# Two layers of a four-mixer decoder trunk: array quarters in C, token forms by TensorE, GpSimd's products on VectorE, and a new instruction order

## The chip, the cores and the metric

The kernel runs on one core of a Trainium2 chip. The metric is the device time of one execution in microseconds (us), the median of several runs. The engines are TensorE (PE in the profile; its weight loads are PEld), VectorE (DVE), ScalarE (ACT), GpSimd (POOL) and SyncE (SP), which issues the DMAs.

## The reference, cut to what matters

Two post-norm layers work on x of 512 tokens by 1024 channels, in float32. One input projection feeds four mixers that stand side by side, each with four heads of 64 channels:

```python
for l in range(DEPTH):                                   # DEPTH = 2
    h = x @ w_in[l]
    o_a = gated_deltanet(...)    # A: conv, chunks of 64, triangular inverse, scan over 8 chunks
    o_b = mla(...)               # B: latent attention, causal softmax, 128-query blocks
    o_c = hgrn2(...)             # C: S_t = diag(f_t) S_{t-1} + (1-f_t) i_t^T, o_t = S_t^T q_t
    o_d = dilated_attention(...) # D: (window, dilation) = (128,1), (512,4), (2048,16), ALiBi
    mixed = concat(o_a, o_b, o_c, o_d) @ w_out[l]
    x = layer_norm(ALPHA * x + mixed)
    x = layer_norm(ALPHA * x + W2 @ square(relu(W1 @ x)))
```

C, linear attention with a decay for each channel, is what the change touches most. Its scores within a chunk of 64 tokens are sums over channels of q_t k_s times the product of the f between s and t.

## The kernel before, in words

**Layout.** Activations are held with channels on the 128 partitions and the 512 tokens along the row. A head has 64 channels, so a row tile holds two heads, called a pair; `p` is 0 or 1 for the two pairs of a mixer, and `half[h]` is the half of the partitions of head `h` in its pair.

**Two kinds of matmul.** Projections, the output projection and the feed-forward go through `mm3` (line 558): each operand is split into a high and a low part of type fp32r (`split`, line 544: ScalarE copies the high part, VectorE subtracts), and three matmuls of 512 columns make one product. All else is plain fp32, for which the trace has two records of a matmul, and one of a transpose.

**An order made by a planner.** Every operation is recorded by `Plan.record` (line 263) and placed by `Plan.order` (line 310), a simulation on the host with costs for each operation, a bias for each stream and engine (`BIAS`), a limit of buffers (41 rows of 128x512, eight PSUM banks) and costs for a change of TensorE's tile form (`LEAVE`, `ENTER`). What comes out is the order in which each engine runs its instructions; an engine's order is strict, so an instruction that waits holds up those behind it. All instructions are emitted from one line, so every row of the profile says L472 and one goes by tile names.

**Mixers.** `a_proj` (line 736) makes A's q, k, v and gate. `to_tokens` (line 587) turns a row tile into its token form, tokens of a chunk on the partitions: eight VectorE transposes of 32x32 blocks, 32 partitions each. It is called for A's v and k (`vtok`, `ktok`) and for C's value and key (`vt`, `kt`). A's triangular inverse is a chain of small VectorE operations (`LB`, `TB`, `W`), spread into `T` and `U` and finished by 64x64 matmuls; `quads` (line 582) writes such a set of sixteen, chunk by chunk, head by head. Since operands and output of head `h` lie on `half[h]`, a set uses two of the array's four 64x64 quarters, those on the diagonal.

C (from line 1047) goes pair by pair, streams C0 and C1. Its scores are made in seven levels, and between levels q and k are multiplied by decay products (`qa` on VectorE, `kr` and `tot` on GpSimd):

```python
quads(p, lambda n, s: pe.matmul(o[s, n], lhsT=v3(kr[p])[s, n], rhs=v3(qa[p])[s, n],
                                start=True, stop=True))
ve.copy_predicated(v3(sc[p]), rep(ci[:, i]), scores())
ve.tensor_tensor(qv[:, :, 1], qv[:, :, 1], spread(tv[:, :, 0], b), OP.mult)
po.tensor_tensor(kv[:, :, 0], kv[:, :, 0], spread(tv[:, :, 1], b), OP.mult)
```

`attend` (line 1152) does one pair of heads and one block of 128 queries in B and D: scores, softmax, transposes on TensorE (`tt`), and value products `out[half[h]]`, 128 rows by 64 columns of the array for each head. In D a score is two fp32r matmuls: `dq` with `dk`, which holds the high part of a head on one half and the low part on the other, on all 128 rows; then the low part of q (`dl`) with `dk` on the head's own 64 rows.

GpSimd does single products of two SBUF tiles: `qd`, `dt`, `db`, `N`, `kd` and the scan's state `st` in A, `t1` and `t2` in B, `fl`, `kr` and `tot` in C, `gm` in `gated` (line 616).

Of the kernel before, what the change touches and what calls it, by code (L numbers as in the profile page):

```python
# [159 lines left out]
class Plan:  # L160
# [4 lines left out]
    TO_PE = 70.0  # L165
    LEAVE, ENTER = 95.0, {(128, 128): 105.0}
    WINDOW, DOWN, UP = 3413.0, 0.29, 0.65

    def __init__(self, nc):
        self.nc, self.ops, self.tiles = nc, [], 0  # L170
        self.kinds, self.queues, self.stream, self.bias = {}, {}, "", 0
        self.quota, self.reserve, self.fifo = {}, {}, set()
        self.ties, self.tied = {}, None
# [33 lines left out]
    def cost(self, e, method, out, ins, k):  # L207
        n = math.prod(out.shape[1:])
        psum = any(v.buf.kind == "ps" for v in [out, *ins])
        if e == "pe":  # L210
            if method == "transpose":
                return 109.0
            w, x = k["lhsT"], k["rhs"]
            n, m = math.prod(x.shape[1:]), w.shape[1]
            if w.dt == FR:
                return max(n * 0.4167 + 13.5, 109.0)
            t = 2 * max(2 * n * 0.4167 + 3, 2 * min(m, n) * 0.4167 + 3, 25.0)
            if w.shape[0] <= 64 or m <= 64:
                return t - 12 if out.span()[0] < 64 else 12.0
            return t  # L220
# [26 lines left out]

    def tile_of(self, method, k):
# [5 lines left out]
        return grid(k["lhsT"].shape[0]), grid(k["lhsT"].shape[1])  # L254

# [7 lines left out]
    def record(self, e, method, a, k):  # L263
# [8 lines left out]
        ins = [v for v in [*a[1:], *k.values()] if isinstance(v, View) and not any(v is o for o in outs)]  # L272
# [32 lines left out]
        if self.tied is not None and e.name == "pe":  # L305
            self.tied.append(i)
        self.ops.append([e, method, a, k, deps, list(bufs.values()), cost, tail, i + self.bias + BIAS.get((self.stream, e.name), 0),
                         self.activity(e, method, k, cost), self.tile_of(method, k)])

    def order(self):  # L310
# [18 lines left out]
        warm, dense, mode, run, forced = False, True, None, 0, None  # L329
# [44 lines left out]
        while done < n:  # L374
            best = None
            for e, cand in avail.items():
                pick = None
                for i in cand if forced is None or e != "pe" else (forced,):
                    t = max(at[e], ready[i])
                    new = [b for b in ops[i][5] if not b.held]  # L380
# [8 lines left out]
                    turn = e == "pe" and mode is not None and ops[i][10] != mode  # L389
                    if turn and at[e] - ready[i] < PATIENCE:  # L390
# [10 lines left out]
            t = max(at[e], ready[i])  # L401
            for kd in {b.kind for b in new}:
# [10 lines left out]
            if e == "pe":  # L413
# [5 lines left out]
                if not warm:  # L419
                    cost, work = 2 * cost, 2 * work  # L420
                if mode is not None and op[10] != mode:
                    t = max(t, at[e] + self.LEAVE)
                    cost += self.ENTER.get(op[10], 50.0)
                mode, forced = op[10], self.ties.get(i)
                run = run + 1 if op[9] >= DENSE else 0
                busy += work
                gap = math.exp(-(t - at[e]) / EMA)
# [3 lines left out]
            at[e] = t + cost  # L431
            self.warm[i] = warm
            end[i] = at[e]
# [9 lines left out]
            for j in users[i]:  # L443
# [6 lines left out]
                ready[j] = max(ready[j], end[i] + lat)  # L450
# [24 lines left out]
def emit(ctx, tc, io, layers=DEPTH):  # L475
# [117 lines left out]

    def tables(first, n, name):
# [14 lines left out]
    for l in range(layers):  # L609
# [6 lines left out]
        def gated(ot, gate, gain, k, tag):  # L616
# [7 lines left out]
            po.tensor_tensor(m, ot, sq, OP.mult)  # L624
# [108 lines left out]
        kq = [big("kq", [128, 8, 2, 64]) for _ in range(2)]  # L733
        vtok, z = [None, None], [None, None]
        bx = row("bx")
        def a_proj(name, o=None):
# [31 lines left out]
            dst = kq[p][:, :, 1 if name[1] == "q" else 0, :]  # L768
# [83 lines left out]
        for p in range(2):  # L852
# [10 lines left out]
            po.tensor_tensor(v3(qd[p]), kq[p][:, :, 1, :], v3(eg), OP.mult)  # L863
# [4 lines left out]
            po.tensor_tensor(v3(dt), v3(dt), rep(incl), OP.mult)  # L868
            db = row("db")
            po.tensor_tensor(v3(db), v3(dt), spread(beta[:, :, p]), OP.mult)  # L870
            QK[p] = row("QK")
            for nh in range(2):
                o = ps("a", (128, 4, 2, 64))
                for i in range(4):
                    for h in range(2):
                        b = kq[p][half[h], 4 * nh + i]
                        pe.matmul(o[half[h], i], lhsT=b[:, 0, :], rhs=b, start=True, stop=True)
# [14 lines left out]
        sq1 = row("bsq1")  # L892
# [6 lines left out]
        ac.activation(cq[1][lo], bx[lo], AF.Copy, scale=pcol(P_GQ + 1, lo))  # L899
        ac.activation(sq1[lo], bx[lo], AF.Square)  # L900
        s = ps("a")
        total(s, oner, [sq, sq1[lo]])
# [3 lines left out]
        for h in range(4):  # L906
# [3 lines left out]
            pe.matmul(o, lhsT=wuq[1][lo, hs], rhs=cq[1][lo], start=False, stop=True)  # L910
# [13 lines left out]
        r = slice(64, 96)  # L924
        t1 = row("t1")
        t2 = row("t2")
        po.tensor_tensor(t1[r], bx[r], qtab[r], OP.mult)
        po.tensor_tensor(t2[r], bx[r], ktab[r], OP.mult)
        o = ps("b")
        pe.matmul(o, lhsT=kdup[r], rhs=t1[r], start=True, stop=False)  # L930
        pe.matmul(o, lhsT=krot[r], rhs=t2[r], start=False, stop=True)
# [44 lines left out]
        for p in range(2):  # L976
# [3 lines left out]
            po.tensor_tensor(Nv, pn(LT, p), rep(lev), OP.mult)  # L980
# [21 lines left out]
            to_tokens(v3(ktok), kq[p][:, :, 0, :])  # L1002
            ve.tensor_tensor(v3(ke), v3(ktok), spread(ce[:, 0, :, p]), OP.mult)
            po.tensor_tensor(v3(kd[p]), v3(ktok), spread(ce[:, 1, :, p]), OP.mult)
# [8 lines left out]
        for n in range(8):  # L1013
# [28 lines left out]
            else:  # L1042
                po.tensor_tensor(new, st, spread(ce[:, 2, n]), OP.mult)
# [22 lines left out]
        for name in W_TILES[9:17]:  # L1066
# [4 lines left out]
            if name[1] == "f":  # L1071
# [4 lines left out]
                po.tensor_tensor(fl, fl, e, OP.add)  # L1076
# [8 lines left out]
            elif name[1] == "i":  # L1085
# [3 lines left out]
                to_tokens(v3(vt[p]), v3(t))  # L1089
# [5 lines left out]

        ot = [row("ot"), row("ot")]
        for p in range(2):
            def scores():
                o = ps("b", (128, 8, 64))
                quads(p, lambda n, s: pe.matmul(o[s, n], lhsT=v3(kr[p])[s, n], rhs=v3(qa[p])[s, n],  # L1100
                                                start=True, stop=True))
                return o
            plan.stream = f"C{p}"
            sc[p] = row("sc")
            ve.tensor_tensor(v3(sc[p]), scores(), rep(id64), OP.mult)
            ve.tensor_tensor(qa[p], qa[p], f[p], OP.mult)
            tot = f[p]
            for i in range(6):
                b = 1 << i
                if i < 4:  # L1110
                    ve.copy_predicated(v3(sc[p]), rep(ci[:, i]), scores())
                else:
                    o = ps("b", (128, 8, 64))
                    parts = [(a, slice(a, a + b), slice(a + b, a + 2 * b)) for a in range(0, 64, 2 * b)]
                    quads(p, lambda n, s: [pe.matmul(o[s.start + a:s.start + a + b, n, cq], lhsT=v3(kr[p])[s, n, ck],
                                                     rhs=v3(qa[p])[s, n, cq], start=True, stop=True)
                                           for a, ck, cq in parts])
# [4 lines left out]
                nb = S // (2 * b)  # L1122
                qv = qa[p].rearrange("q (n s b) -> q n s b", s=2, b=b)
                kv = kr[p].rearrange("q (n s b) -> q n s b", s=2, b=b)
                tv = tot.rearrange("q (n s) -> q n s", s=2)
# [3 lines left out]
                po.tensor_tensor(nt_, tv[:, :, 0], tv[:, :, 1], OP.mult)  # L1129
                tot = nt_  # L1130
            kt = row("kt")
            to_tokens(v3(kt), v3(kr[p]))
            ds_ = ps("b", (128, 8, 64))
            quads(p, lambda n, s: n < 7 and pe.matmul(ds_[s, n], lhsT=v3(kt)[s, n], rhs=v3(vt[p])[s, n],
# [294 lines left out]
```

## Time and profile before

| what | us |
|---|---|
| median of 3 runs | 1382.39 (1381.54 to 1384.11) |
| the profiled execution's own time | 1383.82 |
| its span, first to last instruction | 1382.0 |
| TensorE busy in the span | 1336.3 |
| VectorE busy | 784.7 |
| ScalarE busy | 596.7 |
| GpSimd busy | 91.4 |

The profiled execution has 1.8 us outside the span. In the rows, "busy" joins overlapping instructions. A record of TensorE lasts until its modelled end, so records overlap, and the time that one costs is seen from the start of one to the start of the next. TensorE's granted clock was 0.985 of full speed on average; it has two levels, 2.4 GHz (1.00 in the rows) and 1.2 GHz (0.50).

The mixers of the first layer take the span from about 0 to 297 us, its output projection and feed-forward from there to 669 us; the second layer repeats this from 669 us.

### The profile page before, as it was taken

To read this page: it belongs to the slowest core of one execution; us is meant where nothing else is said; L and a number is where in the kernel's file an instruction comes from. 1 tells how busy PE (TensorE), PEld (TensorE's weight loads), DVE (VectorE), ACT (ScalarE), POOL (GpSimd) and SP (SyncE) were. 2 spreads that over 40 slices of the span, in tenths; PEclk is the share of its full clock that TensorE was granted. 3 is DMA by queue.
4 is the path that set the end of the run, shared out by engine and by line. 5 is a ranking of instruction groups with operands and counts; after the bars stand their busy time and mean duration, and the time that the engine had idled before them with its cause. 6 is when DMAs were issued, how large, how long until landed. Compare 5 with 4: busy or idle time off the path is not lost.

```text
span 1382.0 us, 21797 instructions
## 1 busy us (share of the span) xinstructions
PE 1336.3 (97%) x8860; PEld 1084.0 (78%) x8860; DVE 784.7 (57%) x1533; ACT 596.6 (43%) x1124; POOL 91.4 (7%) x108
## 2 busy tenths in 40 slices
PE   8899999999999999999998989999999999999997
PEld 7657778778888888888886678787788888888886
DVE  6989585567743334422479898846658333344226
ACT  6643456548432223321485434656374322233112
POOL 0222020010000000000003212200000000000000
PEclk9999999999999999999999999999999999999999
DMA  6122201232542223324122242021415323232341
GB/s 225 40 88 77 82 4 47 77 122 74 165 141 93 92 92 94 105 92 155 59 92 62 92 146 71 3 69 69 135 64 189 116 92 92 92 106 92 126 149 61
DMA packets 44164, 132.65 MB, mean 96 GB/s; under 512 B 4896, under 2 KB 5152, under 8 KB 44064
## 3 DMA queue, kind: packets, MB, share of 16 engines
q1 hardware_dynamic: 44064, 131.27, 29.5%
q8 instruction: 69, 1.13, 0.3%
q14 instruction: 31, 0.25, 0.1%
HBM read 122.86 MB, written 8.39 MB: 95 GB/s over the span
## 4 chain that ended last, share of the span: by engine, by line
PE 76%; DVE 14%; ACT 7%; issue 2%; DMA 1%; POOL 0%; SPq 0%; DVEq 0%; POOLq 0%; ACTq 0%
PE mm L472 42%; PE a L472 17%; PE b L472 16%; ACT lny L472 2%; DVE wl L472 1%; DVE xt L472 1%; DVE y L472 1%; ACT wh L472 1%; DVE vtok L472 1%; PE o L472 1%; DVE ktok L472 1%; ACT scr L472 1%; ACT sg L472 1%; ACT xH L472 1%; DVE X L472 1%
## 5 line engine op out<-in xcount | busy, mean ns | idle before, releaser
L472 DVE TENSOR_TENSOR wl<-wr,wh 128x1024 fp32r<-128x1024 f32 (+1 forms) x195 | 237.6, 1222 | 360.4 <-ACT wh L472 355.1
L472 ACT ACTIVATE wh<-wr 128x1024 fp32r<-128x1024 f32 (+1 forms) x195 | 204.7, 1054 | 528.6 <-PE mm L472 501.1
L472 PE MATMUL mm<-xH,wl 128*128 128x512 f32 (+1 forms) x832 | 328.0, 395 | 0.0
L472 PE MATMUL mm<-xL,wh 128*128 128x512 f32 (+1 forms) x832 | 326.6, 393 | 0.0
L472 PE MATMUL mm<-xH,wh 128*128 128x512 f32 (+1 forms) x832 | 325.7, 392 | 0.7 <-DVE as L472 0.4
L472 PEld LDWEIGHTS mm<-xH,wh 128*128 128x128 f32 x832 | 157.9, 190 | 38.1 <-issue 1.9
L472 PEld LDWEIGHTS mm<-xL,wh 128*128 128x128 f32 x832 | 157.5, 190 | 38.1 <-issue 2.3
L472 PEld LDWEIGHTS mm<-xH,wl 128*128 128x128 f32 x832 | 157.6, 190 | 34.8 <-issue 1.6
L472 DVE TENSOR_TENSOR hL<-h,hH 128x512 fp32r<-128x512 f32 x64 | 41.8, 687 | 73.4 <-PE mm L472 73.2
L472 PE MATMUL b<-wh,hL 128*128 128x512 f32 x192 | 74.8, 390 | 0.0
L472 PE MATMUL b<-wh,hH 128*128 128x512 f32 x192 | 74.8, 390 | 0.0
L472 PE MATMUL a<-wh,hH 128*128 128x512 f32 x192 | 74.8, 389 | 0.0
L472 PE MATMUL a<-wl,hH 128*128 128x512 f32 x192 | 74.8, 389 | 0.0
L472 PE MATMUL b<-wl,hH 128*128 128x512 f32 x192 | 74.7, 389 | 0.0
L472 PE MATMUL a<-wh,hL 128*128 128x512 f32 x192 | 74.7, 389 | 0.0
L472 PE MATMUL mm<-wh,hH 128*128 128x512 f32 x128 | 49.9, 390 | 0.0
L472 PE MATMUL mm<-wh,hL 128*128 128x512 f32 x128 | 49.8, 389 | 0.0
L472 PE MATMUL mm<-wl,hH 128*128 128x512 f32 x128 | 49.8, 389 | 0.0
L472 ACT ACTIVATE at<-at,as 128x512 f32<-128x512 f32 (+3 forms) x64 | 35.7, 558 | 27.6 <-DVE as L472 27.5
L472 ACT ACTIVATE hH<-h 128x512 fp32r<-128x512 f32 x64 | 37.3, 619 | 15.4 <-DVE h L472 15.2
L472 DVE TENSOR_TENSOR h<-h,mm 128x512 f32<-128x512 f32 x60 | 40.6, 680 | 3.6 <-ACT h L472 3.6
L472 PEld LDWEIGHTS a<-wl,hH 128*128 128x128 f32 x192 | 36.1, 188 | 7.6
(292 smaller groups left out, 2275.8 us busy)
## 6 DMA issues: line engine op xcount, KB each, us to landing
wr<-in_w_ff_dram SPq DMA_DIRECT2D x128, 512.0 KB, 3.6
wr<-in_w_in_dram SPq DMA_DIRECT2D x47, 512.0 KB, 3.6
wr<-in_w_out_dram SPq DMA_DIRECT2D x16, 512.0 KB, 3.6
x<-xt SPq DMA_DIRECT2D x24, 256.0 KB, 2.1
xt<-x SPq DMA_DIRECT2D x24, 256.0 KB, 5.8
ln<-in_ln_dram SPq DMA_DIRECT2D x16, 256.0 KB, 5.5
x<-in_xT_dram SPq DMA_DIRECT2D x8, 256.0 KB, 6.1
dtab<-in_tabs_dram SPq DMA_DIRECT2D x8, 256.0 KB, 4.0
```

The lines of the kernel that those rows point to most:

```text
L472: getattr(e.real, method)(*[real(v) for v in a], **{n: real(v) for n, v in k.items()})
```

## The change

Six edits:

1. `turn` takes the place of `to_tokens`: four TensorE transposes of 128x128 into one PSUM bank, and four ScalarE copies of 64 partitions by 256 elements out of it. For pair 1 of C the two heads are put on crossed halves.
2. C works both pairs in step. `four` writes a set of matmuls for both pairs, in the order chunk, pair, head, with pair 1's output on the other half of the partitions; `together` ties the set into one uninterrupted run of TensorE. The read-out is split in two: a set with the scores, copied by ScalarE, and for each pair a set with the state, added by VectorE.
3. Value products of a block in `attend` are tied into one run by `together`.
4. D's second score matmul takes all 128 rows: the low part of q is kept once per head and copied to both halves by ScalarE. In B the up-projection of q and the rotary products take 128 rows, and the two squares are added by VectorE ahead of one `total`.
5. All `po.tensor_tensor` become `ve.tensor_tensor`; GpSimd keeps its memsets.
6. The planner has other constants and a finer model: quarters of the array that are free on their own, a port that VectorE and GpSimd share, 21 biases in the place of 4. The order of all instructions is new.

```diff
-FILL = (0.3, 0.5)
-EMA = 2000.0
-BURST = 2
-PATIENCE = 2000.0
+FILL = (0.1, 0.4)
+EMA = 3000.0
+BURST = 4
+PATIENCE = 1000.0
-BIAS = {('A0', 'ac'): -50, ('B', 've'): 600, ('C0', 've'): 200, ('D', 'ac'): -200}
+BIAS = {('', 've'): -550, ('A', 'ac'): 400, ('A', 'po'): 1400, ('A', 've'): -25, ('A0', 'ac'): -250,
...
+    def turn(dst, src, tag, crossed=0):
+        o = ps(tag, (128, NT, 128))
+        for m in range(NT):
+            pe.transpose(o[:, m], src[:, 128 * m:128 * m + 128], ident)
+        d = dst.rearrange("q (m c) i -> q m c i", c=2)
+        for h in range(2):
+            for c in range(2):
+                ac.activation(d[half[h ^ crossed], :, c], o[half[c], :, 64 * h:64 * h + 64], AF.Copy)
...
-                to_tokens(v3(vtok[p]), v3(y))
+                turn(v3(vtok[p]), y, "a")
...
-            po.tensor_tensor(v3(qd[p]), kq[p][:, :, 1, :], v3(eg), OP.mult)
+            ve.tensor_tensor(v3(qd[p]), kq[p][:, 1], v3(eg), OP.mult)
...
+        ve.tensor_tensor(sq[lo], sq[lo], sq1[lo], OP.add)
         s = ps("a")
-        total(s, oner, [sq, sq1[lo]])
+        total(s, oner, [sq])
...
-            pe.matmul(o, lhsT=wuq[1][lo, hs], rhs=cq[1][lo], start=False, stop=True)
+            pe.matmul(o, lhsT=wuq[1][:, hs], rhs=cq[1], start=False, stop=True)
...
-        for p in range(2):
-            def scores():
-                o = ps("b", (128, 8, 64))
-                quads(p, lambda n, s: pe.matmul(o[s, n], lhsT=v3(kr[p])[s, n], rhs=v3(qa[p])[s, n],
-                                                start=True, stop=True))
-                return o
...
+        def four(tags, fn, chunks=8):
+            o = [ps(tags, (128, 8, 64)) for p in range(2)]
+            with plan.together():
+                for n in range(chunks):
+                    for p in range(2):
+                        for h in range(2):
+                            fn(o[p], p, n, half[h], half[h ^ p])
+            return o
+
+        def level(o, p, n, s, x):
+            pe.matmul(o[x, n], lhsT=v3(kr[p])[s, n], rhs=v3(qa[p])[s, n], start=True, stop=True)
...
+                for p, o in enumerate(four("b", level)):
+                    ve.copy_predicated(v3(sc[p]), rep(ci[:, i]), o)
...
-                po.tensor_tensor(kv[:, :, 0], kv[:, :, 0], spread(tv[:, :, 1], b), OP.mult)
+                ve.tensor_tensor(kv[:, :, 0], kv[:, :, 0], spread(tv[:, :, 1], b), OP.mult)
...
+        inner = four("b", lambda o, p, n, s, x: pe.matmul(
+            o[s, n], lhsT=v3(vt[p])[x, n], rhs=v3(sc[p])[x, n], start=True, stop=True))
+        for p in range(2):
+            ac.activation(ot[p], inner[p].rearrange("q n i -> q (n i)"), AF.Copy)
             o = ps("b", (128, 8, 64))
+            quads(p, lambda n, s: n and pe.matmul(o[s, n], lhsT=sv[p][s, n], rhs=v3(qa[p])[s, n], start=True, stop=True))
+            ve.tensor_tensor(v3(ot[p])[:, 1:], v3(ot[p])[:, 1:], o[:, 1:], OP.add)
...
-            for j in range(n + 1):
-                for h in range(2):
-                    pe.matmul(out[half[h]], lhsT=vv[j // 2][:, j % 2, 64 * h:64 * h + 64], rhs=tt[h][:, 128 * j:128 * j + 128],
-                              start=j == 0, stop=j == n)
+            with plan.together():
+                for j in range(n + 1):
+                    for h in range(2):
+                        pe.matmul(out[half[h]], lhsT=vv[j // 2][:, j % 2, 64 * h:64 * h + 64],
+                                  rhs=tt[h][:, 128 * j:128 * j + 128], start=j == 0, stop=j == n)
...
-                    ve.scalar_tensor_tensor(dl[p][a], o[a], -0.125, t[a].bitcast(FT), op0=OP.mult, op1=OP.subtract)
+                    r = dl[2 * p + h] = row("dl", FR)
+                    ve.scalar_tensor_tensor(r[a], o[a], -0.125, t[a].bitcast(FT), op0=OP.mult, op1=OP.subtract)
+                    ac.activation(r[b], r[a].bitcast(FT), AF.Copy)
...
-                a = half[i % 2]
-                pe.matmul(o, lhsT=dl[i // 2][a, qs], rhs=dk[i][a, ks], start=False, stop=True)
+                pe.matmul(o, lhsT=dl[i][:, qs], rhs=dk[i][:, ks], start=False, stop=True)
```

## Rows read from the trace of the kernel before

**Rows 1.** The page: the span and each engine's busy time, share and instructions.

```profile
span 1382.0 us, 21797 instructions
PE 1336.3 (97%) x8860; PEld 1084.0 (78%) x8860; DVE 784.7 (57%) x1533; ACT 596.6 (43%) x1124; POOL 91.4 (7%) x108
```

**Rows 2.** Windows: length, busy us (instructions) per engine, granted clock, DMA share, GB/s.

```profile
40.00:127.00 87.00, 79.61 (x375) 57.06 (x373) 81.33 (x158) 41.92 (x67) 26.86 (x28) 0.96 0.24 75
160.00:220.00 60.00, 57.00 (x1054) 44.31 (x1055) 49.14 (x144) 32.89 (x96) 12.54 (x17) 1.00 0.04 14
345.00:669.00 324.00, 324.00 (x1468) 267.06 (x1467) 122.65 (x141) 97.00 (x127) 0.00 (x0) 1.00 0.36 115
720.00:814.00 94.00, 87.61 (x409) 63.23 (x407) 87.57 (x172) 46.90 (x74) 23.57 (x20) 0.96 0.24 75
63.60:70.40 6.80, 5.68 (x12) 3.64 (x12) 6.77 (x10) 0.00 (x0) 2.20 (x2) 0.50 0.22 77
128.40:135.30 6.90, 5.75 (x108) 5.75 (x109) 4.89 (x11) 2.25 (x3) 0.00 (x0) 0.51 0.01 3
```

**Rows 3.** TensorE's timeline in C: start us, duration us, what, count of records.

```profile
178.76 0.80 PE L472 MATMUL b<-qa,kr 64*64 64x64 f32 x21
...
887.46 0.69 PE L472 MATMUL b<-qa,kr 64*16 64x16 f32 x64
```

**Rows 4.** Groups of TensorE by form: records, busy us, mean ns, idle before.

```profile
L472 PE MATMUL b<-qa,kr 64*64 64x64 f32 x640 | 28.9, 225 | 0.4 <-DVE as L472 0.2
...
L472 PE MATMUL b<-tt,bv 128*64 128x128 f32 x160 | 14.4, 282 | 0.8 <-ACT tt L472 0.5 <-DVE as L472 0.2
...
L472 PE MATMUL b<-tt,dv 128*64 128x128 f32 x160 | 13.4, 278 | 0.0
...
L472 PE MATMUL a<-sqh,oner 64*128 64x512 f32 x2 | 1.3, 645 | 0.0
```

**Rows 5.** TensorE's timeline at D's value products.

```profile
268.40 2.18 PE L472 MATMUL b<-tt,dv 128*64 128x128 f32 x18
...
274.19 1.31 PE L472 MATMUL b<-tt,dv 128*64 128x128 f32 x20
```

**Rows 6.** TensorE's timeline: projections of 256 columns, then D's scores of 256.

```profile
249.35 0.28 PE L472 MATMUL mm<-wl,xH 128*128 128x256 f32 x1
249.47 0.28 PE L472 MATMUL mm<-wh,xL 128*128 128x256 f32 x1
...
254.40 0.38 PE L472 MATMUL a<-dk,dl 64*128 64x256 f32 x1
254.71 0.38 PE L472 MATMUL a<-dk,dq 128*128 128x256 f32 x1
```

**Rows 7.** TensorE's timeline at the softmax transposes.

```profile
263.01 1.25 PE L472 MATMUL b<-cc,at 128*128 128x128 f32 x10
```

**Rows 8.** Waits of TensorE: total us, times, longest us.

```profile
PE a L472 <- DVE sql L472: 7.7, 4, 3.1
PE a L472 <- DVE T L472: 7.0, 4, 2.0
...
PE b L472 <- DVE qh L472: 2.9, 1, 2.9
```

**Rows 9.** Groups of VectorE by form.

```profile
L472 DVE STREAM_TRANSPOSE ktok<-kq 32x256 f32<-32x256 f32 x32 | 13.9, 436 | 0.6
...
L472 DVE TENSOR_TENSOR qa<-qa,tot 128x256 f32<-128x256 f32 x20 | 10.5, 527 | 2.9 <-PE b L472 2.8
...
L472 DVE TENSOR_TENSOR ke<-ktok,ce 128x512 f32<-128x512 f32 x4 | 7.0, 1761 | 0.0
...
L472 DVE TENSOR_TENSOR U<-U,a 128x512 f32<-128x512 f32 x4 | 2.7, 681 | 0.4 <-PE a L472 0.4
```

**Rows 10.** Groups of GpSimd by form.

```profile
L472 POOL TENSOR_TENSOR kr<-kr,tot 128x256 f32<-128x256 f32 x20 | 15.2, 764 | 50.9 <-PE b L472 50.8
```

**Rows 11.** Groups of ScalarE by form.

```profile
L472 ACT ACTIVATE Y<-a 32x256 f32<-32x256 f32 x8 | 3.0, 375 | 6.1 <-PE a L472 6.0
```

More of the change, by code (lines that the diff above doesn't have):

```diff
@@ L172, in __init__ @@
         self.quota, self.reserve, self.fifo = {}, {}, set()
-        self.ties, self.tied = {}, None
+        self.ties, self.tied, self.streams = {}, None, []
     @contextmanager
@@ L246, in cost, with shares @@
         return 450.0
+    def shares(self, e, method, ins, out):
+        inside = [v for v in ins if v.buf.kind != "ps"]
+        if e == "po":
+            return bool(inside)
+        if e != "ve":
+            return False
+        return len(inside) > 1 or (method in ("tensor_scalar", "tensor_copy") and len(inside) == 1 and out.buf.kind != "ps")
     def tile_of(self, method, k):
@@ L254, in tile_of, with cells, streaming @@
         return grid(k["lhsT"].shape[0]), grid(k["lhsT"].shape[1])
+    def cells(self, method, a, k):
+        if method == "transpose":
+            return tuple(range(16))
+        rows, cols = self.tile_of(method, k)
+        r, c = k["lhsT"].span()[0] // 32, a[0].span()[0] // 32
+        return tuple(4 * i + j for i in range(r, r + rows // 32) for j in range(c, c + cols // 32))
+    def streaming(self, e, method, k):
+        if e.name != "pe":
+            return 0.0
+        if method == "transpose":
+            return 107.0
+        w, n = k["lhsT"], math.prod(k["rhs"].shape[1:])
+        return n * 0.4167 * (1 if w.dt == FR else 4) * w.shape[0] / 128
     def activity(self, e, method, k, cost):
@@ L271, in record @@
             outs.append(k["accum_out"])
-        ins = [v for v in [*a[1:], *k.values()] if isinstance(v, View) and not any(v is o for o in outs)]
+        ins = [v for v in [*a[1:7], *(v for w, v in k.items() if w not in ("out", "accum_out"))] if isinstance(v, View)]
         if method == "copy_predicated" or (method == "matmul" and not k["start"]):
@@ L389, in order @@
                     turn = e == "pe" and mode is not None and ops[i][10] != mode
+                    if e == "pe":
+                        t = max(t, drained) if turn else max(t, max(free[c] for c in ops[i][12]))
                     if turn and at[e] - ready[i] < PATIENCE:
@@ L1088, in emit @@
                 vt[p] = row("vt")
-                to_tokens(v3(vt[p]), v3(t))
+                turn(v3(vt[p]), t, "b", p)
             else:
@@ L1094, in emit @@
                 silu(t, gz[p])
+        plan.stream = "C"
         ot = [row("ot"), row("ot")]
-        for p in range(2):
-            def scores():
-                o = ps("b", (128, 8, 64))
-                quads(p, lambda n, s: pe.matmul(o[s, n], lhsT=v3(kr[p])[s, n], rhs=v3(qa[p])[s, n],
-                                                start=True, stop=True))
-                return o
-            plan.stream = f"C{p}"
-            sc[p] = row("sc")
-            ve.tensor_tensor(v3(sc[p]), scores(), rep(id64), OP.mult)
-            ve.tensor_tensor(qa[p], qa[p], f[p], OP.mult)
[L1107 to L1117, printed above, removed]
@@ new lines, in emit, with blocks_of @@
+        tot = list(f)
+        for p, o in enumerate(four("b", level)):
+            ve.tensor_tensor(v3(sc[p]), o, rep(id64), OP.mult)
+        for p in range(2):
+            ve.tensor_tensor(qa[p], qa[p], f[p], OP.mult)
+        for i in range(6):
+            b = 1 << i
+            if i < 4:
+                for p, o in enumerate(four("b", level)):
+                    ve.copy_predicated(v3(sc[p]), rep(ci[:, i]), o)
+            else:
+                parts = [(a, slice(a, a + b), slice(a + b, a + 2 * b)) for a in range(0, 64, 2 * b)]
+                def blocks_of(o, p, n, s, x):
+                    for a, ck, cq in parts:
+                        pe.matmul(o[x.start + a:x.start + a + b, n, cq], lhsT=v3(kr[p])[s, n, ck],
+                                  rhs=v3(qa[p])[s, n, cq], start=True, stop=True)
+                for p, o in enumerate(four("b", blocks_of)):
@@ L1128, in emit @@
                 nt_ = plan.tile("row" if nb > 64 else "sm", [128, nb], FT, "tot")
[L1129 to L1134, printed above, removed]
-                                                      start=True, stop=True))
-            sn = row("sn")
@@ L1147, in emit @@
-            quads(p, read)
-            ac.activation(v3(ot[p]), o, AF.Copy)
+                ve.tensor_tensor(nt_, tv[:, :, 0], tv[:, :, 1], OP.mult)
+                tot[p] = nt_
+        kt, sv = [row("kt"), row("kt")], [v3(row("sn")), v3(row("sn"))]
+        for p in range(2):
+            turn(v3(kt[p]), kr[p], "b", p)
+        for p, o in enumerate(four("b", lambda o, p, n, s, x: pe.matmul(
+                o[s, n], lhsT=v3(kt[p])[x, n], rhs=v3(vt[p])[x, n], start=True, stop=True), 7)):
+            ve.tensor_copy(sv[p][:, 1], o[:, 0])
+            for n in range(1, 7):
+                ve.scalar_tensor_tensor(sv[p][:, n + 1], sv[p][:, n], tot[p][:, n:n + 1], o[:, n], op0=OP.mult, op1=OP.add)
@@ L1149, in emit @@
+        for p in range(2):
             gated(ot[p], gz[p], P_GC, 4 + p, "b")
```

94 lines of the change are left out of this document (52 added, 42 removed), and 4 rows, old and new, of the table BIAS.

## The prediction

> **What bounds the kernel now.** I read the page first: TensorE is busy 97% of the span, VectorE 57%, ScalarE 43%, GpSimd 7% [rows 1]. TensorE's records overlap, so 97% is no proof that it is full; the windows by stage come next. The feed-forward (324 us in each layer) keeps TensorE at 324.00 of 324.00 and is touched by nothing here [rows 2]. What can move is the mixers, some 300 us in each layer, and they are two kinds of stretch. In A's preparation (40 to 127 us, and 720 to 814 in the second layer) VectorE is busy 81.3 of 87 and 87.6 of 94 us: it sets the pace, and TensorE fills in with projections. In A's scan, C's levels and B's attention (160 to 220) VectorE has 49 of 60 us and TensorE 57 of 60, nearly all of it small fp32 matmuls at full clock: here TensorE sets it. So the reader should see two bounds, and an edit is worth what it takes from the one that holds in its place. Last, TensorE's waits: those for VectorE's `sql`, `T` and `qh`, all in A's preparation, are 17.6 us [rows 8]. The clock falls there: two stretches of 6.8 us stand at 0.50 [rows 2], two more like them lie in the second layer, 27 us together.
>
> **TensorE, edit by edit** (both layers).
>
> *Quarters in C.* A run of 21 records of a level takes 0.80 us. Less the last one's own 0.225 [rows 4] that is 0.575 over 20 steps, 29 ns a record, with two quarters at work [rows 3]. Four make it 14.5 if nothing else limits: the 16-column form takes at most 0.69/64 = 11 ns a record with its weight load [rows 3], so issue and loading allow it. By the code the edit reaches 640 records of the scores, 112 of the state products and 128 of the read-out: 880 x 14.5 ns = 12.8 us. The bounds are 0 (quarters that share rows don't overlap) and -12.8; I take -12, as the issue row is nearest. The 16- and 32-column levels use more than two parts of the array already; nothing.
>
> One rule of the Trainium skill speaks against this term. The row shows both diagonal quarters writing one PSUM bank and still 58 ns for a pair of records [rows 3]. The page "TensorEngine Tiling (Array Packing)", Restrictions and Gotchas, says that different row tiles cannot access one PSUM bank at the same time; in the change each bank is again written from both row halves. By that rule the term would be 0 in place of -12. The trace does not agree with it for two quarters, and nothing here shows four.
>
> *Value products.* Twenty records in pairs take 1.31 us, 54 ns each after the last one's 0.278; eighteen out of pairs 2.18, or 112 [rows 5]. The 320 records of B and D are busy 27.8 us [rows 4]; all paired, 17.3. The difference of 10.5 holds entries and waits too, and many are paired now: bounds 0 and -10.5, I take -6.
>
> *D's second score matmul.* Two 256-column matmuls that change the tile form start 0.31 us apart, without a change 0.12 [rows 6]: 0.19 for a change. Of the 64 score matmuls the wide ones run in sets, the 256-column ones and part of the 128 alternate; some 24 changes go: -4.6, bounds 0 and -12.2 (64 of them). The added rows cost nothing, a matmul's time going by its columns.
>
> *B.* Two records of a 64-row `total` go and two like them: four at up to 0.645 us [rows 4]; up to eight changes of form go with the rotary and up-projection products: -2.5, bounds 0 and -4.1.
>
> *Token forms.* Ten transposes take 1.25 us, 0.107 each after the last one's overlap [rows 7]. Sixteen calls of four are 64: +6.8. `ktok` and `kt` stand among 64-row work, eight calls with up to two changes of form at 0.19: at most +3.0. I take +8.5, between +6.8 and +9.8.
>
> Sum for TensorE: -12 - 6 - 4.6 - 2.5 + 8.5 = -16.6 us.
>
> **VectorE, ScalarE, GpSimd.** A call of `to_tokens` is eight transposes at 0.436 us [rows 9], 3.5 us; sixteen calls are 55.8 us off VectorE. In A's preparation `vtok` and `ktok` are 32 transposes, -14.0 us a layer. To it come `qd`, `dt`, `db`, `N`, `kd` twice each, B's two rotary products and the addition of squares: 13 x 0.681 [rows 9] = +8.9. VectorE is also held up by GpSimd: `ke`, the same size and form as the 0.681 row, takes 1.761 [rows 9] while GpSimd runs; twice 1.08 us come back at least. GpSimd is busy 26.9 us of that stretch [rows 2], so it may be several times that; I put 10 as the most. VectorE gets 7 to 15 us shorter of 81, in each layer.
>
> In C's stretch `vt` and `kt` take another 14.0 off, and `kr` comes in with 12 x 0.527 [rows 9], where GpSimd took 0.764 [rows 10], `fl`, `gm` and the addition of the read-out with six of 0.681, and eighteen small products (`tot`, `st`) that I estimate at 0.2 to 0.3 from the 0.527 of 256 columns: about 15. Even, so VectorE stays at some 49 of 60 us and does not become the bound there. The step also changes shape: a level's set waits for `qa` and `kr` of both pairs, then takes 64 x 14.5 ns = 0.9 us, while VectorE needs for both pairs about 2 x (0.681 + 0.527 + 0.527 + 0.2) = 3.9. Six such steps are 29 us of a stretch of 60. TensorE's cover for the rest is A's scan and B's attention; without it three of four microseconds of a level are idle, up to 18 us a layer.
>
> ScalarE gets 64 copies; the nearest row, 32 x 256 out of PSUM, is 0.375 [rows 11]: +24 us, and eight copies for `dl`. With 42 of 87 busy [rows 2] it has room, but a copy queues behind weight splits, and `turn` is then late for what reads it: the transposes and copies of a call need about 2 us after the last input, still under the 3.5.
>
> So the waits of 17.6 us and half of the 27 us at half clock, 31 us in all, are exposed to a VectorE that finishes 7 to 15 us earlier in stretches where it was late by 3 us at a time. The new order may spend the slack on something else; I take -12, between 0 and -31. Where these waits go, TensorE's own work is next: it has few idle stretches left there.
>
> **New order.** Its other effects I can't read from the trace: zero, with 15 us either way.
>
> **Sum.** -16.6 - 12 = -28.6 us against the profiled execution's own 1383.8: 1355.2. The median of the runs lies 1.4 us lower: **1354 us**.
>
> **Rivals.**
> *Quarters that don't overlap (0.11).* The rule above as a mechanism: a second pair in the array waits for the first, a level's set takes 1.9 us and C keeps TensorE as it is: 1354 + 12 = 1366. For it: no row shows more than two 64-column streams. Against it: the pair on one bank.
> *The waits stay (0.12).* A's chain (`LB`, `TB`, `T`) is a sequence whose length, not VectorE's load, sets when `T` comes, and 13 more products now stand in the same queue ahead of it. Then 12 us are not had: 1366, and if the chain grows by the 8.9 us in both layers, 1383 at worst. For it: 0.94 busy leaves no room to jump the queue. Against it: 14.0 go out of the same queue.
> *More than that (0.13).* All 31 us of waits and half clock go: 1335.
> *Slower, by the clock (0.13).* The clock stands at 0.50 after TensorE had waited for VectorE, and at 1.00 from 160 to 220, where it has 57 of 60 us of work [rows 2]. The change takes 8 to 10 us of that work out of each such stretch, leaves VectorE as it is and ties C's sets, so TensorE waits between them. If the clock falls there, each microsecond at half clock costs up to 0.5. It decides from 57 us more of half clock on, half of the two stretches; both whole, with TensorE the limit for two thirds of them, cost 0.5 x 120 x 2/3 = 40: 1394. Against it: the waits in A that now pull the clock down get shorter. The page "TensorE: Matmul & The Clock Gate", Part 4, says that transposes don't count as work for the clock; 64 more, in groups of 0.43 us, would by themselves move it little, and that rule has no run here to agree with.
> *No change to speak of (0.04)*: gains and new waits cancel.
>
> **How the numbers follow.** The forecast has 0.47, with its own range of 1340 to 1366. A run here tells 0.2%, 2.8 us, from no change. Faster: forecast 0.47, "more" 0.13, the first two rivals 0.23 less 0.02 for their worst ends: 0.81. Slower 0.13 and what spills over: 0.14. Same 0.05. For 8 in 10 I leave out the slow rival's tail above 1386 and half of "more" below 1332: **1332 to 1386**.
>
> **What would show it.** Starts of `qa`/`kr` records at about 14.5 ns instead of 29; no 64 x 128 form; value products in runs near 54 ns; 64 transpose records more, no `STREAM_TRANSPOSE` on `vtok`, `ktok`, `vt`, `kt`; `ke` near 0.68; waits for `sql`, `T`, `qh` under 10 us. The prediction is wrong if the granted clock falls in C's stretch, if TensorE waits there for `kr` or `sc`, or if A's preparation is no shorter.

## The result, and the profile after

The changed kernel takes 1336.5 us (median of 4 runs, 1334.9 to 1337.9) against 1382.6 for the kernel before (four runs; the table of before has three of them): a ratio of 0.9665, 95% interval 0.9649 to 0.9682, or 46.1 us less. The forecast was 1354; the time lies below its own range of 1340 to 1366, inside the range of 1332 to 1386, and next to the rival "more than that" (1335).

The page of the profile after, its first lines, in the columns of [rows 1]:

```profile
span 1333.1 us, 21834 instructions
PE 1305.4 (98%) x8920; PEld 1060.9 (80%) x8920; DVE 741.6 (56%) x1505; ACT 620.8 (47%) x1194; POOL 4.8 (0%) x12
```

TensorE idles 27.7 us of its span (1333.1 less 1305.4) where it idled 45.7, and its mean granted clock is 0.996 where it was 0.985. Windows, columns as in [rows 2]:

```profile
40.00:127.00 87.00, 85.88 (x815) 65.70 (x813) 74.11 (x164) 50.58 (x93) 1.85 (x2) 1.00 0.26 80
160.00:220.00 60.00, 57.61 (x842) 44.70 (x841) 47.23 (x137) 44.86 (x110) 0.00 (x0) 1.00 0.10 30
267.00:271.50 4.50, 3.80 (x12) 2.83 (x11) 1.48 (x3) 0.28 (x1) 0.00 (x0) 0.62 0.30 115
690.00:770.00 80.00, 78.71 (x431) 58.31 (x431) 73.80 (x156) 53.38 (x96) 0.00 (x0) 1.00 0.26 80
```

In A's preparation (the first line) TensorE now works 85.9 of 87 us at full clock, with 815 records where there were 375 (part of them A's inverse, whose first product `T`,`N` starts at 107.0 us and started at 127.4); VectorE is down from 81.3 to 74.1. C's stretch kept its 57 of 60 at full clock. Apart from the last microseconds of the span, where TensorE has ended, two stretches at half clock are left, of 3.4 us each; the third line holds the first of them. TensorE's waits say the same [rows 8]: `sql` and `qh` are gone, `T` is down from 7.0. One sign that the prediction named against itself is there, small: in C of the second layer TensorE waits once for `kr`.

```profile
PE a L522 <- ACT wh L522: 5.3, 1, 5.3
PE o L522 <- DVE mixL L522: 2.3, 3, 0.9
PE a L522 <- DVE xt L522: 2.1, 6, 0.5
PE a L522 <- DVE T L522: 1.6, 3, 0.9
...
PE b L522 <- DVE kr L522: 1.2, 1, 1.2
```

TensorE's timeline at the token forms, C and D of the first layer (start, duration, what, records), to be read against [rows 3, 5, 6]:

```profile
69.68 0.66 PE L522 MATMUL a<-cc,y 128*128 128x128 f32 x4
...
163.69 1.16 PE L522 MATMUL b<-qa,kr 64*64 64x64 f32 x64
...
179.86 1.22 PE L522 MATMUL b<-qa,kr 64*16 64x16 f32 x128
...
192.17 1.04 PE L522 MATMUL b<-vt,kt 64*64 64x64 f32 x56
...
196.39 3.42 PE L522 MATMUL b<-qa,sn 64*64 64x64 f32 x56
...
242.48 2.62 PE L522 MATMUL b<-tt,dv 128*64 128x128 f32 x44
...
248.84 0.28 PE L522 MATMUL a<-dk,dq 128*128 128x256 f32 x1
248.96 0.28 PE L522 MATMUL a<-dk,dl 128*128 128x256 f32 x1
```

A set for both pairs is 64 records in 1.16 us: less the last one's own 0.220, 63 steps of 14.9 ns. The set that reads the state (`qa`,`sn`) stands by itself now; it takes 3.42 us for 56 records, because it starts before VectorE has all states (in the kernel with two quarters below, where they are all there, it takes 1.85). The last three lines are D: 44 value records in one run, 54 ns a step as in the better run of [rows 5], and the two score matmuls 0.12 us apart, without a change of form [rows 6]. The first line is one call of `turn`: four transposes in 0.66 us.

Groups by form, TensorE, VectorE and ScalarE (busy us, mean ns), against [rows 4, 9, 11]:

```profile
L522 PE MATMUL b<-qa,kr 64*64 64x64 f32 x640 | 12.5, 220 | 1.0 <-DVE as L522 0.9
L522 PE MATMUL b<-tt,bv 128*64 128x128 f32 x160 | 11.6, 280 | 1.0 <-issue 1.0
L522 PE MATMUL b<-tt,dv 128*64 128x128 f32 x160 | 11.2, 280 | 0.7 <-ACT tt L522 0.7
...
L522 DVE TENSOR_TENSOR kr<-kr,tot 128x256 f32<-128x256 f32 x20 | 8.5, 423 | 0.0
L522 DVE TENSOR_TENSOR qa<-qa,tot 128x256 f32<-128x256 f32 x20 | 8.4, 421 | 3.5 <-PE b L522 3.5
L522 DVE TENSOR_TENSOR ke<-ktok,ce 128x512 f32<-128x512 f32 x4 | 2.8, 689 | 0.4 <-ACT ce L522 0.3
...
L522 ACT ACTIVATE kt<-b 64x256 f32<-64x256 f32 x16 | 6.1, 379 | 1.3 <-PE b L522 1.1
```

`ke` is at 0.689 us as estimated, the 256-column products at 0.42 where 0.527 was taken, the copies of `turn` at 0.38.

Where the time came from, worked out by charging each TensorE record the time until the next one starts (waits, changes of form and half clock fall to the record before them; the sum is the span):

| TensorE's records | before | after | less |
|---|---|---|---|
| C: scores, state, inner and read-out products | 43.9 | 25.9 | 18.0 |
| value products of B and D | 26.6 | 24.8 | 1.8 |
| D's scores | 16.5 | 12.0 | 4.5 |
| B's up- and rotary products | 24.4 | 20.9 | 3.5 |
| transposes of the token forms | 0 | 6.6 | -6.6 |
| 512-column projections and first feed-forward product | 570.2 | 559.5 | 10.7 |
| A's inverse | 28.7 | 23.8 | 5.0 |
| sums of squares (`sqh`, `sql`) | 12.9 | 8.0 | 4.9 |
| softmax transposes, B's scores, A's preparation | 63.2 | 55.1 | 8.1 |
| all else | 595.6 | 596.5 | -0.9 |

The first five lines are the work that the edits touch, with the waits and changes of form that fall to it: 21.2 us less. The next four have the same records as before, apart from four fewer in the sums, and are 28.7 us shorter: waits, clock and changes of form.

### The profile page after: what moved, and what is told of

It reads as the page before. It is cut to its first block, busy times and chain, and to the rows that moved or that the text cites. A ratio compares the mean times of both kernels' runs of the same rounds, so it can differ in the third digit from the quotient of the medians.

```text
span 1333.1 us, 21834 instructions
## 1 busy us (share of the span) xinstructions
PE 1305.4 (98%) x8920; PEld 1060.9 (80%) x8920; DVE 741.6 (56%) x1505; ACT 620.8 (47%) x1194; POOL 4.8 (0%) x12
## 4 chain that ended last, share of the span: by engine, by line
PE 82%; DVE 8%; ACT 7%; issue 1%; DMA 1%; DVEq 0%; SPq 0%; ACTq 0%
PE mm L522 47%; PE a L522 19%; PE b L522 15%; ACT lny L522 2%; DVE xt L522 2%; PE o L522 1%; ACT wh L522 1%; DVE wl L522 1%; DVE U L522 1%; ACT scr L522 1%; ACT xH L522 1%; DVE T L522 1%; DMA ln<-in_ln_dram 0%; DVE sn L522 0%; ACT kt L522 0%
## 5 line engine op out<-in xcount | busy, mean ns | idle before, releaser
L522 DVE TENSOR_TENSOR hL<-h,hH 128x512 fp32r<-128x512 f32 x64 | 43.9, 692 | 73.3 <-PE mm L522 70.6
L522 ACT ACTIVATE hH<-h 128x512 fp32r<-128x512 f32 x64 | 40.5, 632 | 93.4 <-PE mm L522 73.7
L522 ACT ACTIVATE at<-at,as 128x512 f32<-128x512 f32 (+3 forms) x64 | 35.7, 559 | 21.4 <-DVE as L522 21.3
L522 PEld LDWEIGHTS a<-wh,hH 128*128 128x128 f32 x192 | 36.0, 188 | 7.6
```

The source lines that it names most:

```text
L522: getattr(e.real, method)(*[real(v) for v in a], **{n: real(v) for n, v in k.items()})
```

## The experiments

Theory 1: the edits do it, TensorE by shorter sets and VectorE by the token forms, and the order adds little. Theory 2: the new planner, with 21 biases where there were four, does it. "Own order" below means that the changed kernel's order is kept instruction for instruction, and only the instructions of the edit are put in the place of others; the diffs of these kernels are shortened to what the replaced instructions become. A ratio is to the kernel before, measured beside the experiment. The kernel before took 1381.6 to 1383.0 us in these comparisons, so a difference between two of them is good to some 1.5 us.

**Edits or order.** Three kernels swap the planner's part of the file (constants and `Plan`) and the rest.

```diff
 # old planner: FILL, EMA, BURST, PATIENCE, BIAS and Plan of before; emit() of after
-BIAS = {('', 've'): -550, ('A', 'ac'): 400,
...
+BIAS = {('A0', 'ac'): -50, ('B', 've'): 600, ('C0', 've'): 200, ('D', 'ac'): -200}
 # new planner: the same the other way round, emit() of before
 # four biases: the changed kernel with this one edit of BIAS alone
```

> All edits of the change, ordered by the planner of before with its constants and 4 biases. Theory 1 (the edits bring the time, any planner can harvest it): 1340 to 1358 us, at least 25 of the 46 us kept. Theory 2 (the new order brings it): 1365 us or more, with TensorE's waits for sql, T and qh back near 17 us and two or more stretches at half clock in A's preparation.

> The operations of before, ordered by the new planner with its constants and 21 biases. Theory 1 (edits): within 15 us of before, 1367 us or more. Theory 2 (order): 1355 us or less with the same operations.

> The operations of the change and the finer planner, but with the 4 biases of before. The old planner on the same operations gave 1349.7 us and the whole change 1336.5. If the finer model is what finds the order: 1336 to 1341. If the 21 biases are: 1345 to 1352.

All edits under the old planner: 1349.7 us (ratio 0.9772, interval 0.9756 to 0.9788), clock 0.996 as with the new one. The old operations under the new planner: 1375.7 (0.9956, 0.9941 to 0.9971). All edits under the finer planner with four biases: 1353.2 (0.979, 0.9775 to 0.9804). So with four biases the edits bring 33 of the 46 us under the old planner and 29 under the finer one, as theory 1 has it. The other 13 come with the new planner, as theory 2 has it, and they need its 21 biases: without them the finer model is 3.5 us slower than the old planner, just above the 1345 to 1352 us expected for that case. The planner alone, on the old operations, brings 6. Under it the old operations trade waits. The lines of its list of waits:

```profile
PE b L522 <- POOL t L522: 9.2, 2, 5.2
PE a L522 <- ACT sqh L522: 6.0, 3, 3.5
...
PE a L522 <- DVE T L522: 2.5, 3, 1.1
```

`T` is down, and GpSimd's rotary product and the sums of squares are late in its place.

**Two quarters or four.** Own order; in `four`, pair 1 of C goes back on the diagonal, its crossed halves in `turn` too.

```diff
-                            fn(o[p], p, n, half[h], half[h ^ p])
+                            fn(o[p], p, n, half[h], half[h])
```

> The changed kernel in its own order, instruction for instruction; only pair 1 of C is put back on the diagonal quarters, so that a level's set uses two quarters of the array in the place of four. If the quarters are worth what their records cost: 64 records of a set go from 14.9 to about 29 ns each, 880 records in all, +11 to +13 us. Rival (C's sets wait for VectorE anyway, and the quarters only give TensorE idle time): +4 us or less.

1343.5 us (0.9723, 0.9709 to 0.9738), 7.0 more than with four, between theory and rival. The same sets in the timeline:

```profile
165.83 2.08 PE L540 MATMUL b<-qa,kr 64*64 64x64 f32 x64
...
202.33 1.85 PE L540 MATMUL b<-qa,sn 64*64 64x64 f32 x56
```

63 steps of 29.5 ns, twice 14.9. By the accounting above scores, inner and state products are 12.3 us longer, and the read-out is 2.2 shorter: with slower sets the states are there in time and the set runs through in 1.85. The quarters overlap in full, and 5 of their 12 us are not seen in the time: 2.2 of them go into the read-out's wait for VectorE, the rest in parts too small to place. With two quarters the table's first line is 36.0 us (25.9 + 12.3 - 2.2), so 7.9 of its 18.0 come without the quarters, by the uninterrupted sets, the split read-out or the order; these were not separated.

**64-row forms.** Own order; D's second score and B's rotary and second up-projection products are put back on 64 and 32 rows.

```diff
-                pe.matmul(o, lhsT=dl[i][:, qs], rhs=dk[i][:, ks], start=False, stop=True)
+                pe.matmul(o, lhsT=dl[i][a, qs], rhs=dk[i][a, ks], start=False, stop=True)
...
-        pe.matmul(o, lhsT=kdup, rhs=t1, start=True, stop=False)
+        pe.matmul(o, lhsT=kdup[r], rhs=t1[r], start=True, stop=False)
```

> The changed kernel in its own order; only D's second score matmul is put back on 64 rows, and B's second up-projection and rotary matmuls on 64 and 32 rows. If each change of the tile form costs 0.19 us as the rows of before showed it: the order of the change alternates the two score matmuls, so up to 64 changes come back in D and some 12 in B, +5 to +13 us. Rival (a change of form is hidden in waits for VectorE's softmax): +2 us or less.

1352.6 us (0.9785, 0.977 to 0.98), 16.0 more, and more than the theory's 13. TensorE's timeline at D's scores:

```profile
254.33 0.28 PE L540 MATMUL a<-dk,dq 128*128 128x256 f32 x1
254.54 0.38 PE L540 MATMUL a<-dk,dl 64*128 64x256 f32 x1
...
257.03 0.38 PE L540 MATMUL a<-dk,dq 128*128 128x256 f32 x1
257.35 0.38 PE L540 MATMUL a<-dk,dl 64*128 64x256 f32 x1
```

The starts are 0.21 to 0.32 us apart where they were 0.12. Counted over the trace, TensorE changes its form 234 times where the changed kernel does so 151 times: 83 more for 16.0 us, 0.19 each, which is the price that the prediction read from [rows 6]. Part of that is no longer the change itself: by the accounting D's scores are 7.7 and B's up- and rotary products 5.0 us longer, 0.15 a change, and the two stretches at half clock last 6.8 us each where they lasted 3.4.

**Token forms and GpSimd's products, each and both.** First in the own order: the products back on GpSimd, the token forms back on VectorE (without TensorE's 64 transposes and ScalarE's copies), and both.

```diff
-                ve.tensor_tensor(kv[:, :, 0], kv[:, :, 0], spread(tv[:, :, 1], b), OP.mult)
+                po.tensor_tensor(kv[:, :, 0], kv[:, :, 0], spread(tv[:, :, 1], b), OP.mult)
 # and the eleven others
-            turn(v3(kt[p]), kr[p], "b", p)
+            to_tokens(v3(kt[p]), v3(kr[p]), p)
 # and the three others
```

> The changed kernel in its own order; only the products of two SBUF tiles (qd, dt, db, N, kd, st, t1, t2, fl, kr, tot, gm) are run by GpSimd again. Theory 1 (VectorE's freedom from GpSimd shortens A's preparation): +8 to +20 us, ke again over 1.5 us, T later by 5 us or more in each layer. Rival (the load that these products put on VectorE is as bad as GpSimd was): within 3 us of the changed kernel.

> The changed kernel in its own order; only the token forms are made by eight VectorE transposes again, in the places of the four ScalarE copies; TensorE's 64 transposes are left out. If VectorE's load sets the pace of A's preparation: 28 us a layer come back on VectorE, 6.6 us go from TensorE, +8 to +25 us in all. Rival (TensorE's order alone sets the time): 3 to 7 us faster than the changed kernel.

> The changed kernel in its own order with both of the last two put back: the products on GpSimd (alone 10.8 us slower) and the token forms on VectorE. If the two are loads that add up on one engine: the sum of the two alone, within 4 us. Rival (GpSimd and VectorE hold each other up, so that together they cost more): over the sum by 6 us or more.

Products back: 1347.4 us (0.9752, 0.9737 to 0.9766), +10.8. Theory 1 has the time, but not the signs that it named: `ke` stays at 0.689 and `T` is not late. What its trace shows is that the VectorE instructions that both kernels have take 22.5 us more in sum, beside GpSimd's products, and that TensorE's waits for `sqh` are 4.4 us where 0.8 were left. Token forms back: 1375.3 (0.9946, 0.9929 to 0.9963), +38.8, beyond what either theory gave it. Both: 1377.7 (0.9965, 0.9952 to 0.9978), +41.1, below the sum of 49.6, where neither theory had it: once the token forms are back, the products cost only 2.3. The second kernel has the fixed order against it, so three more let the planner adapt: the changed kernel with the token forms on VectorE and the new planner, and the kernel before, under its own planner, with the token forms alone and with the products alone.

```diff
 # changed kernel, planned anew: turn(dst, src, tag, crossed) calls
+        to_tokens(dst, v3(src), crossed)
 # kernel before, first: turn() for to_tokens(), and kq as [128, 2, 8, 64]
-            to_tokens(v3(kt), v3(kr[p]))
+            turn(v3(kt), kr[p], "b")
 # kernel before, second: all twelve po.tensor_tensor
-            po.tensor_tensor(Nv, pn(LT, p), rep(lev), OP.mult)
+            ve.tensor_tensor(Nv, pn(LT, p), rep(lev), OP.mult)
```

> The changed kernel with its new planner and its 21 biases, but the token forms by VectorE again and no transposes or copies of them by TensorE and ScalarE; unlike in the earlier run with the same edit, the order is planned anew with the edit in it. Theory 1 (most of the 38.8 us of the earlier run was the fixed order, which had no place for 56 us more on VectorE): a new order recovers half or more of it, 1345 to 1357 us. Rival (the token forms are worth that much wherever they are planned, since VectorE sets the pace in A's preparation): 1365 to 1378 us, with TensorE's waits for VectorE back.

> The kernel before with its own planner and one edit alone: the token forms by TensorE's transposes and ScalarE's copies. Theory 1 (VectorE's 14 us per layer in A's preparation stood on the path): TensorE does 8 us more and waits and clock give back more than that, 1362 to 1374 us. Rival (TensorE is full, the waits move elsewhere): 1385 to 1391 us, the 64 transposes and some changes of the tile form added.

> The kernel before with its own planner and one edit alone: all of GpSimd's products on VectorE. Theory 1 (GpSimd's run of long instructions and its holding up of VectorE cost more than the products themselves): 1370 to 1379 us, and the 1.761 us row of ke falls to 0.7. Rival (VectorE, without the relief of the token forms, gets 9 us longer per layer in A's preparation and sets the end): 1385 to 1400 us.

All edits but the token forms, planned anew: 1363.7 us (0.9862, 0.9848 to 0.9877). The token forms alone: 1376.0 (0.995, 0.9936 to 0.9965). The products alone: 1394.8 (1.0094, 1.0077 to 1.011), slower. The first two came out between theory and rival, the third as its rival had it, although `ke` fell to 0.683 as its theory said. The window of A's preparation and the longest waits of TensorE, kernel by kernel. All edits but the token forms:

```profile
40.00:127.00 87.00, 73.07 (x632) 54.22 (x631) 82.53 (x186) 38.85 (x67) 1.85 (x2) 0.92 0.17 56
```

```profile
PE a L522 <- ACT sqh L522: 23.4, 4, 12.5
```

What stands before the longest of these waits, from the timeline of all engines:

```profile
77.79 3.58 DVE L522 STREAM_TRANSPOSE vtok<-y 32x256 f32<-32x256 f32 x8
...
86.08 0.44 DVE L522 STREAM_TRANSPOSE ktok<-kq 32x256 f32<-32x256 f32 x1
...
86.68 0.68 DVE L522 TENSOR_TENSOR bsq<-bsq,bsq 64x512 f32<-64x512 f32 x1
87.39 0.63 ACT L522 ACTIVATE sqh<-bsq 128x512 fp32r<-128x512 f32 x1 [11.61 <-DVE bsq L522]
...
88.07 0.79 PE L522 MATMUL a<-sqh,oner 128*128 128x512 f32 x1 [12.51 <-ACT sqh L522]
```

The token forms alone:

```profile
40.00:127.00 87.00, 80.77 (x667) 59.27 (x665) 70.98 (x132) 48.67 (x87) 23.95 (x26) 0.96 0.25 79
```

```profile
PE a L472 <- DVE T L472: 5.7, 3, 2.2
...
PE a L472 <- ACT f L472: 3.0, 1, 3.0
```

The products alone:

```profile
40.00:127.00 87.00, 72.67 (x482) 50.88 (x482) 83.08 (x186) 38.55 (x64) 0.00 (x0) 0.88 0.21 67
```

```profile
PE a L472 <- DVE sql L472: 17.5, 4, 13.0
```

These rows show VectorE at 82 to 83 of 87 us where it has both the transposes and the products, with TensorE waiting 12.5 or 13.0 us at one stretch and the clock at 0.88 to 0.92. Without the token forms the 23.4 us of waits for `sqh` are most of the 27.2 by which this kernel is slower than the changed one. In the longest, VectorE's addition of B's squares (edit 4) stands in its queue behind `vtok`, `ktok` and A's chain; the transposes are 5.3 of the 12.5 us, so the place that the planner gave the addition has a part in it too. With the token forms alone the rows show VectorE relieved to 71 and still 8.7 us of waits for `T` and `f`, in a kernel whose TensorE has got more work (220 changes of form where it had 189). The token forms alone give 7.1 us, all the rest without them (the new planner and its biases included) 19.3, and all together 46.1: 19.7 us belong to neither but to both at once. One rival to this stands untested: the 21 biases are the same in both kernels of the new planner, and may suit the whole change and not the change without its token forms; other biases could then give back part of the 19.7.

**The read-out, later.** The set that waits for VectorE's states looked like a loss of 2 us. In each layer its 28 matmuls were moved behind the next four or five wide matmuls and two softmax transposes of TensorE's queue, and nothing else.

```diff
-            getattr(e.real, method)(*[real(v) for v in a], **{n: real(v) for n, v in k.items()})
+            if not go: continue          # held back by later(), issued after the wide ones
+            getattr(e.real, method)(*[real(v) for v in a], **{n: real(v) for n, v in k.items()})
```

> The changed kernel in its own order, but in each layer the 28 matmuls that read C's state move behind the next five or six wide projection matmuls of TensorE's queue (nothing else moves). In the changed kernel this set starts before VectorE's chain of states is done and takes 3.42 us in the first layer and 2.49 in the second, 1.85 when all states are there. Theory 1 (the set holds up TensorE's queue by what it waits): 1.0 to 2.0 us faster than the changed kernel, 1334.5 to 1335.5. Rival (the waiting time is taken up by the next wait, that for the sums of the gated output): 1336.5, no difference.

1341.2 us (1338.6 to 1341.3; ratio to the kernel before 0.9696, 0.9681 to 0.971): no gain, and above all runs of the changed kernel. TensorE's timeline in its first layer:

```profile
197.70 0.40 PE L522 MATMUL mm<-xH,wh 128*128 128x512 f32 x1
200.22 0.41 PE L522 MATMUL b<-cc,at 128*128 128x128 f32 x2 [2.12 <-DVE at L522]
200.56 2.66 PE L522 MATMUL b<-qa,sn 64*64 64x64 f32 x56
204.24 0.84 PE L522 MATMUL b<-cc,at 128*128 128x128 f32 x2 [1.02 <-DVE as L522]
204.73 0.77 PE L522 MATMUL mm<-xL,wh 128*128 128x512 f32 x1
205.30 0.63 PE L522 MATMUL mm<-xH,wl 128*128 128x512 f32 x1
```

```profile
200.00:210.00 10.00, 8.76 (x86) 7.20 (x87) 4.99 (x15) 6.14 (x15) 0.00 (x0) 0.66 0.00 0
```

TensorE now runs out of wide work before VectorE is through its 2.4 us of states; the softmax results behind them in VectorE's queue are late (2.12 and 1.02 us), and the window shows the clock at 0.66. Both theories were wrong: the stuttering set had kept TensorE working while it waited.

## Why the prediction came out as it did

**Quarters, -12:** right. The records are worth 12.3 us by the kernel with two quarters, 0.9 of it in the 32-column level, which I had put at nothing. Each bank is written from both row halves at 14.9 ns a record, and the rule of the Trainium skill that spoke against it ("TensorEngine Tiling (Array Packing)", Restrictions and Gotchas: different row tiles cannot access one PSUM bank at the same time), by which the set would have stayed at 2.08 us, is not what the trace shows. In the time they are worth 7.0. For the other 7.9 us that C's sets lost there was no term.

**Value products, -6:** mis-sized, -1.8 by the starts. The busy sum fell by 5.0 us [rows 4], but it held overlapped ends; by their starts 246 of the 320 records ran in pairs already, and 316 do after.

**D's second score, -4.6, and B, -2.5:** the price of 0.19 a change was near (0.15 to 0.19) and the count too low for this order: -4.5 and -3.5 in the accounting, but 16.0 when both are put back with the order kept, since 83 changes come with them where I had counted about 32.

**Token forms on TensorE, +8.5:** 6.6 by the starts.

**Waits and clock, -12 between 0 and -31, and the new order, 0 with 15 either way:** these two were mis-sized most, and nearly all of the 17.5 us by which the forecast missed lies in them. The kernel with all edits under the old planner separates them. In its trace the five lines of edited work are 15.4 us shorter than before (16.6 were forecast) and the rest of the span 19.2 (12 were forecast); TensorE's idle time is 32.9 us, and the clock is at 0.996 already. The new order then takes 13.2 us more, within its bounds, where I had put nothing: by the accounting of the two traces 5.8 in the edited lines and 8.5 in the rest. In the changed kernel the idle time has fallen by 18.0 us in all, and of the 17.6 of `sql`, `T` and `qh` 1.6 are left.

Why the relief is worth more than a part of those waits, the kernels without the token forms show: with the transposes on VectorE the sums of squares come late by 12.5 us in one stretch. So the relief decides over more than the waits of 3 us that the profile of before showed: over long ones that come out once TensorE's own work is shorter.

**Rivals.** "More than that" has the number, 1335, but not by its own mechanism alone: under the old planner the rest of the span gives 19.2 of the 31 us that it counts on, and the new order, of which it said nothing, brings the sum there. That it fits so closely is luck. Quarters overlap; the clock in C's stretch did not fall (1.00 from 160 to 220); "the waits stay" is what the products alone do: in the preparation of A and B 12 products a layer, put into VectorE's queue without taking the transposes out, make the kernel 11.8 us slower. That the products pay, 10.8 us in the own order, rests on the token forms: with these back on VectorE it is 2.3.

What is left open: how the interaction of 19.7 us divides between waits and clock, and how much of it is the biases, which were not chosen anew without the token forms; which of the 21 biases carry the 13 us; and what the value products and C's uninterrupted sets are worth each by itself. None of these was tried.

## What to carry to other kernels

When two engines are both near their limit in turn, price an edit with the others in place: here one part alone gave 7 us, another alone lost 12, and together with the rest they gave 46. Here part of that may belong to an order that was planned for the whole. Keep the order fixed to measure a part by itself, and let it be planned anew to learn what the part is worth; the two answers differed by 12 us for the token forms. A set that waits in small steps may be the cheapest place to wait: before it is moved, look at what the engine meets next.

## What the runs showed of the hardware

- Four 64x64 quarters take fp32 records at 14.9 ns each and two at 29.5, into one bank per pair; the 64x16 form with four quarters ran 128 records in 1.22 us, (1.22 - 0.178)/127 = 8.2 ns a step with the weight loads, so issuing them does not set the 14.9.
- A change of TensorE's tile form cost 0.15 us in the records beside it, and 0.19 with all that followed, over 83 of them.
- `ke` took 1.75 to 1.77 us each of four times in the kernel before and 0.689 after. Each of the four began while GpSimd ran `dt` or `qd` and ended 0.54 to 0.55 us after that product did. With the token forms alone, GpSimd still at work, it took 0.680, and with the products back in the own order 0.689: there a product of GpSimd that ran as `ke` began ended 0.03 us later. In these rows VectorE is held up where such a product is already running. Over the whole kernel this is more than `ke`: the VectorE instructions that both kernels have take 21.4 us less in sum with the products alone on VectorE than in the kernel before, some 8 a layer of it in the preparation of A and B, inside the 2.2 to 10 of the prediction. The products' own times on VectorE add up to 44 us, and VectorE's busy time, which joins overlaps, rose all the same, from 784.7 to 797.0.
- The clock fell after short idles in a row: at 267.98 us in the changed kernel, after four waits of 0.94, 0.37, 0.37 and 0.70 us within 4 us, the wide matmuls' starts went from 0.23 to 0.43 us apart for 3.5 us. The 64 transposes more did not lower it: the mean rose to 0.996.
